# Loads for the adaLN steps from GpSimd's queue during scan and attention, and the scan's transposes one piece later

## The chip, the cores and the metric

The kernel runs on one core of a Trainium2 chip. A core has five engines that run their own instruction streams in order and wait for each other through semaphores: TensorE (PE in the profile, with its weight loads as PEld), VectorE (DVE), ScalarE (ACT), GpSimd (POOL) and SyncE (SP, which only issues DMAs). DMAs can be issued from SP, ACT and POOL; an issuing instruction stands in that engine's stream like any other, so what follows it on the same engine comes after it. The metric is the time of one execution on the device, in microseconds.

## What the reference computes

One inference step of a small hybrid network with two layers, 1024 features, 128 context tokens and 512 latent tokens, all in float32. What matters here lies in layer 0:

- adaLN: from a condition vector, `mod = silu(cond) @ w_ada + b_ada` gives shift, scale and gate for the mixer and the FFN of each layer. `w_ada` has 1024 x 6144 numbers for each of the two layers; the result is needed for two conditions (latent and context).
- the even mixer: multi-head latent attention (8 heads, softmax over 640 keys for latent tokens and 128 for context tokens) beside a gated DeltaNet scan in both directions (8 heads, chunks of 64 tokens). The scan's outputs are normalised per head, multiplied with a SiLU gate and go, beside the attention's, through one output projection.
- then SwiGLU, and layer 1 with an mLSTM mixer and another SwiGLU, which the change does not touch.

## The kernel before

The 640 tokens are held feature-major (128 features on the partitions, tokens along the row). Large matrix products are made from two parts of each weight and operand and run on PE at almost full occupancy for most of the execution. One stretch is different: from about 303 to 560 us, after the input projection of layer 0 and before its output projection. There four kinds of work are interleaved by Python generators:

- `expand` (`mla_expand`): for each tile of 128 tokens the up-projections for q, k and v (L1607), norms with a power on POOL (L1656, L1706), and two pieces later the transposes of the result (`emit_T`, L1623), copied by ACT into one staging tile `st` (L1630, one buffer) and stored from there by a DMA on SP's queue into `qTd` or `kTd` (L1632).
- `heads` (`mla_heads`): 16 blocks of two heads and 128 queries, in two pieces each: scores (L1774, L1781), row maxima on DVE (L1776, L1783), exponentials on ACT (L1787), transposes (L1791), product with v (L1804), and a factor spread on POOL (`rbc`, L1801) that a last product uses (L1806).
- `steps` (`chain`): the scan, in 20 pieces. Each two pieces are one chunk step; at its start two DMAs on SP's queue load its matrices into a tile `J` of two buffers (L1514), POOL scales the state (`S`, L1524), and PE and DVE alternate (L1540, L1555, L1565, L1577 on PE). After pieces 8 and 16 and at the end, `delta` handles the outputs of the tiles that are complete: it adds the directions (L1248), loads the gate from `gzd` by a DMA on SP's queue (L1251), squares on ACT (L1255), reduces on DVE (L1257 to L1259), takes a power on POOL (`fac`, L1261), multiplies on DVE (`on`, L1262 and L1263), transposes on PE (L1269) and multiplies the gate in from PSUM on DVE (L1270).
- `ada_more`: one adaLN step and the loads for the next. A step is four matmuls of 256 columns (L500) on one 128 x 1024 block of `w_ada`, which one DMA of 512 KB brings (L483 for the first two sixths of a layer, L486 for the rest). 52 of the 96 blocks come in earlier stages, into a tile `wa`. The other 44 are loaded in this stretch, into the three buffers `wr` that also take the large products' weights (L291). A load waits until the buffer's last reader is done: for an adaLN block that is its step on PE.

The order in the program is given by `run`, which takes one piece of the attention, one `ada_more` and one piece of the chain, over and over: 6 rounds with `expand` and 32 with `heads`, 38 in all. The chain gives way 33 times in it, so it ends in the 34th round. What is left of the adaLN steps follows behind the rounds, and in the tail two splits of the attention's and the scan's outputs feed the output projection (L371 from 560 us on).

The order on each engine is fixed before the kernel runs: a planner of the framework goes through the program with a timing model of its own and lets an engine take, among what is ready at its simulated time, what stands first in the program. What a piece issues may therefore stand earlier or later on its engine than the text of the kernel suggests, and the engines keep that order whatever the chip's real times are.

The lines that set the rounds and a load's place are these:

```python
def ada_more(s):
    if s.aw:
        s.ada_done()
        with s.tc.issue_after(s.gate.ins) if s.gate else nullcontext():
            s.ada_step(1)
    s.ada_load(2 - len(s.aw))
...
run(expand, steps, 1, 1, s.ada_more)
...
run(heads, steps, 1, 1, s.ada_more)
```

Of the kernel before, what the change touches and what calls it, by code (L numbers as in the profile page):

```python
# [214 lines left out]
class K:  # L215
# [28 lines left out]
    def c(s, n):  # L244
        gn, o, w = CONST_COLS[n]
        return s.groups[gn][:, o:o + w]
# [213 lines left out]

    def ada_init(s):
        nc = s.nc
        cs = s.t(s.base, [P, KD, 32], "cond", 1)
        nc.sync.dma_start(cs, s.I["cond"])
        s.cs = cs
        nc.scalar.activation(s.cs, cs, AF.Silu)
        s.ada = [s.t(s.base, [P, 48, 2], f"ada{l}", 1) for l in range(2)]
        s.sw = {}
# [5 lines left out]
    def ada_load(s, n):  # L474
        nc = s.nc
        while s.loads and n:
            n -= 1
            l, b, k = s.loads.pop(0)
            w = s.t(*s.wa)
            src = s.I["w_ada"][l, k]  # L480
            if b < 2:

                s.loaded = nc.sync.dma_start(w.rearrange("p (j n) -> p j n", j=2),  # L483
                                             src[:, :2048].rearrange("p (j n) -> p j n", j=2)[:, :, b * 512:(b + 1) * 512])
            else:
                s.loaded = nc.sync.dma_start(w, src[:, b * 1024:(b + 1) * 1024])  # L486
            s.aw.append(w)

    def ada_step(s, n=1):
# [357 lines left out]
def body(nc, tc, I, O, dbg=None):  # L847
    with ExitStack() as es:
        s = K(nc, tc, I, O, es, dbg)
        s.plan = plan(I)  # L850
        s.ada_init()
        s.ada_start()
        X, norm, e0 = even_mixer(s)
        x1, xw = ExitStack(), ExitStack()

        def nxt():
            return Norm(s, X, s.scale_w(1, 1, s.p("nmix")[:, 8:16]), s.vec(1, 0), s.pool("oh", 1, x1, side="right"), xw, "ow")
        norm = s.ffn(0, X, norm, e0, nxt)
        X, norm, e1 = odd_mixer(s, X, norm, x1, xw)
        s.ffn(1, X, norm, e1)  # L860
        for k in range(KD - 1):
            nc.sync.dma_start(O["yT"][:, k, :], X[:, k, :])
        for n in range(2):
            nc.sync.dma_start(O["yT"][:, KD - 1, 320 * n:320 * n + 320], X[:, KD - 1, 320 * n:320 * n + 320])


def even_mixer(s):
    nc, I, O = s.nc, s.I, s.O
# [7 lines left out]
    with ExitStack() as es:  # L876
# [16 lines left out]
        with ExitStack() as en:  # L893
# [50 lines left out]
            for n in ("qnr", "knr"):  # L944
                cw = s.t(bp, [P, 6, 32], "cw" + n, 1)
                sw = s.t(bp, [P, 6, 2, 2, 8], "sw" + n, 1)
                w = s.p(n)
# [26 lines left out]
        with ExitStack() as ec:  # L974
# [249 lines left out]
            for hf in range(2):  # L1224
# [3 lines left out]
                nc.vector.tensor_copy(SM[r, 8 + hf], K3[r, :, 0, 4])  # L1228
                nc.vector.tensor_copy(SM[r, 9 - hf], K3[r, :, 1, 4])
        s.wa = s.w, [P, 1024], "wr", WR  # L1230
        eh.close()

        US = [Bg[i // 4][:, (i % 4) * 8:(i % 4) * 8 + 8, :].rearrange("p s d -> p (s d)") for i in range(10)]
# [6 lines left out]
        def delta(ts):  # L1240

            on = {}
            for t in ts:
                o, sq = s.t(fp, [P, 512], "o", 2), s.t(fp, [P, 512], "on", 2)
                for hf in range(2):
                    r = slice(64 * hf, 64 * hf + 64)
                    sf, sb = (2 * t + hf, 7 - 2 * t - hf) if t < 4 else (8 + hf, 9 - hf)
                    nc.vector.tensor_add(o[r], US[sf][r], US[sb][r])  # L1248
                on[t] = o, sq
            for t in ts:  # L1250
                nc.sync.dma_start(zt[t].rearrange("p (b k) -> p b k", b=4), gzd[:, :, t * P:(t + 1) * P])  # L1251
            yield 1
            for t in ts:
                o, sq = on[t]
                nc.scalar.activation(sq, o, AF.Square)  # L1255
                red = s.t(fp, [P, 8], "red", 2)
                nc.vector.tensor_reduce(out=red, in_=sq.rearrange("p (s d) -> p s d", s=8), axis=AX.X, op=ALU.add)  # L1257
                nc.vector.tensor_tensor(red, red, f2[:, t, :], op=ALU.mult)
                nc.vector.tensor_scalar(red, red, 1.0 / 64 / 64, EPS, op0=ALU.mult, op1=ALU.add)  # L1259
                fac = s.t(fp, [P, 8], "fac", 2)  # L1260
                nc.gpsimd.tensor_tensor(fac, red, c("mhalf")[:, :8], op=ALU.pow)  # L1261
                nc.vector.scalar_tensor_tensor(fac, in0=fac, scalar=0.125, in1=rq[:, t, :], op0=ALU.mult, op1=ALU.mult)  # L1262
                nc.vector.tensor_tensor(sq.rearrange("p (b a d) -> p a b d", a=2, b=4), o.rearrange("p (a b d) -> p a b d", a=2, b=4),  # L1263
                                        fac.rearrange("p (a b) -> p a b", a=2).unsqueeze(3).to_broadcast([P, 2, 4, 64]), op=ALU.mult)
                yield 1
            for t in ts:
                pt = s.p1()
                for b in range(4):
                    nc.tensor.transpose(pt[:, b * P:(b + 1) * P], on[t][1][:, b * P:(b + 1) * P], c("ident"))  # L1269
                nc.vector.scalar_tensor_tensor(zt[t], in0=pt, scalar=won, in1=zt[t], op0=ALU.mult, op1=ALU.mult)  # L1270
                yield 1

        def chain(pool):
            for n, _ in enumerate(scan(s, pool, qk, SM, EGL, scr, US)):
                yield 1
                if n in (7, 15):
                    yield from delta((4,) if n == 7 else (1, 2))
            yield from delta((0, 3))
# [894 lines left out]
```

## Time and profile before

| | |
|---|---|
| median of 3 runs | 1830.22 us (1830.02 to 1830.99) |
| the profiled execution | 1834.05 us, span from first to last instruction 1832.3 us |
| mean granted clock of TensorE | 0.974 of full speed |
| busy share of the span: PE, PEld, DVE, ACT, POOL | 95%, 88%, 63%, 41%, 22% |
| HBM traffic | 115 GB/s over the span |
| stretch 303 to 560 us: busy PE, DVE, ACT, POOL | 234.68, 153.80, 107.26, 42.70 us of 257 |

The span leaves out 1.75 us of the profiled execution, which lies 3.83 us above the median of the unprofiled runs. The granted clock takes one of two levels, full speed (2.4 GHz, written 1.00) and half of it (1.2 GHz, written 0.50); a window that holds both shows a mean.

### The profile page before, as it was taken

What the parts mean: (1) busy time and instruction counts of PE and PEld (TensorE: products, weight loads), DVE (VectorE), ACT (ScalarE), POOL (GpSimd) and SP (SyncE); (2) the same over time, 40 slices, a digit from 0 to 9 for tenths busy, and PEclk for the clock granted to TensorE, in tenths of its full rate; (3) what the DMA queues carried; (4) which work ended last, traced back from release to release, by engine and by line L of the source; (5) the groups of instructions that cost most, each with busy time, mean ns of one, the idle gap of its engine ahead of it and who ended that gap; (6) DMA issues with size and microseconds to landing.
All of it is one profiled execution on the core that took longest, in us unless ns stands there. A gap on an engine that the chain in (4) does not pass through costs nothing.

```text
span 1832.3 us, 34561 instructions
## 1 busy us (share of the span) xinstructions
PE 1748.9 (95%) x14159; PEld 1615.2 (88%) x14159; DVE 1155.8 (63%) x2217; ACT 756.7 (41%) x1472; POOL 397.4 (22%) x334
## 2 busy tenths in 40 slices
PE   5999988898999989999999999999998999999999
PEld 3888877665669989999999999988998999999999
DVE  5568997465664688458538573544657873684573
ACT  3454435432434555235415343621426451452251
POOL 2026323211110124124123000022301421340330
PEclk9999997899999999999999999999999999999999
DMA  9576542785733222323312334421321232233122
GB/s 367 167 215 203 188 131 97 203 243 158 196 116 106 59 68 83 95 67 84 102 58 84 114 108 118 127 75 53 104 73 45 90 94 82 70 87 98 58 78 84
DMA packets 96163, 212.90 MB, mean 116 GB/s; under 512 B 7964, under 2 KB 41436, under 8 KB 94596
## 3 DMA queue, kind: packets, MB, share of 16 engines
q1 hardware_dynamic: 92980, 205.37, 36.4%
q10 hardware_dynamic: 3024, 5.32, 1.1%
q8 instruction: 111, 1.82, 0.4%
q14 instruction: 48, 0.39, 0.1%
HBM read 189.91 MB, written 20.75 MB: 115 GB/s over the span
## 4 chain that ended last, share of the span: by engine, by line
PE 80%; DVE 8%; DMA 5%; ACT 3%; issue 2%; SPq 1%; POOL 1%; ACTq 0%; DVEq 0%; POOLq 0%
PE mm L371 30%; PE p L352 18%; PE mm L352 12%; PE pa L500 2%; PE p L1781 2%; PE p L401 1%; PE p L1804 1%; DVE tmp L1413 1%; PE p L2044 1%; PE p L1791 1%; PE p L1607 1%; DMA wr<-in_w_ada 1%; ACT hf L789 1%; SPq L1940 1%; DMA D<-grd 1%
## 5 line engine op out<-in xcount | busy, mean ns | idle before, releaser
L286 ACT CAST wp<-wr 128x1024 fp32r<-128x1024 f32 (+2 forms) x224 | 188.0, 840 | 486.5 <-PE mm L371 350.0
L371 PE MATMUL mm<-hi,wp 128*128 128x320 f32 x1696 | 330.9, 313 | 1.5 <-DVE x L544 0.7
L287 DVE TENSOR_TENSOR wp<-wr,wp 128x1024 fp32r<-128x1024 f32 (+2 forms) x220 | 256.8, 1169 | 74.7 <-ACT wp L286 67.6
L371 PE MATMUL mm<-hf,wp 128*128 128x320 f32 x1836 | 278.7, 310 | 0.6 <-DVE x L544 0.4
L371 PEld LDWEIGHTS mm<-hi,wp 128*128 128x128 f32 x1696 | 266.6, 188 | 14.1 <-issue 8.5
L371 PEld LDWEIGHTS mm<-hf,wp 128*128 128x128 f32 x1836 | 273.2, 189 | 1.1 <-PE mm L371 1.1
L371 PE MATMUL mm<-lo,wp 128*128 128x320 f32 x848 | 196.7, 311 | 0.0
L544 DVE SCALAR_TENSOR_TENSOR x<-mm,ada,x 128x320 f32<-128x320 f32 (+2 forms) x174 | 66.2, 434 | 201.2 <-PE mm L371 191.6
L352 PE MATMUL p<-T,wp 128*128 128x320 f32 x1164 | 185.8, 308 | 0.0
L352 PEld LDWEIGHTS p<-T,wp 128*128 128x128 f32 x1164 | 174.6, 188 | 0.0
L287 DVE TENSOR_TENSOR wp<-st,wp 128x512 fp32r<-128x512 f32 x160 | 135.1, 866 | 22.7 <-ACT wp L286 21.3
L352 PE MATMUL p<-B,wp 128*128 128x320 f32 x864 | 143.9, 309 | 1.9 <-ACT wp L286 1.9
L371 PEld LDWEIGHTS mm<-lo,wp 128*128 128x128 f32 x848 | 142.2, 188 | 1.2 <-issue 0.4
L286 ACT CAST wp<-st 128x512 fp32r<-128x512 f32 x160 | 95.7, 621 | 100.3 <-PE p L352 42.8
L312 POOL TENSOR_TENSOR st<-st,wr 128x512 f32<-128x512 f32 x40 | 54.0, 1351 | 382.4 <-DMA wr<-in_w_fi 107.9
L352 PEld LDWEIGHTS p<-B,wp 128*128 128x128 f32 x864 | 131.0, 188 | 2.5 <-ACT wp L286 2.5
L352 PE MATMUL mm<-T,wp 128*128 128x320 f32 x756 | 119.9, 308 | 0.0
L352 PEld LDWEIGHTS mm<-T,wp 128*128 128x128 f32 x756 | 113.2, 187 | 0.0
L352 PE MATMUL mm<-B,wp 128*128 128x320 f32 x576 | 95.4, 309 | 0.9 <-ACT wp L286 0.9
L352 PEld LDWEIGHTS mm<-B,wp 128*128 128x128 f32 x576 | 87.3, 188 | 1.2 <-ACT wp L286 1.2
L312 POOL TENSOR_TENSOR st<-wr,st 128x512 f32<-128x512 f32 x40 | 69.9, 1747 | 6.9 <-DVE wp L287 6.2
L623 POOL TENSOR_TENSOR a<-a,p 128x320 f32<-128x320 f32 x40 | 37.9, 948 | 145.7 <-DVE p L584 144.6
(511 smaller groups left out, 2818.1 us busy)
## 6 DMA issues: line engine op xcount, KB each, us to landing
wr<-in_w_fi SPq DMA_DIRECT2D x68, 512.0 KB, 3.6
wa<-in_w_ada SPq DMA_DIRECT2D x52, 512.0 KB, 5.6
wr<-in_w_ada SPq DMA_DIRECT2D x44, 512.0 KB, 4.5
wr<-in_w_fo SPq DMA_DIRECT2D x32, 512.0 KB, 3.5
wr<-in_w_odd SPq DMA_DIRECT2D x25, 512.0 KB, 3.6
wr<-in_w_even SPq DMA_DIRECT2D x22, 512.0 KB, 4.9
J<-scr SPq DMA_DIRECT2D x20, 512.0 KB, 7.6
w<-in_w_fi SPq DMA_DIRECT2D x20, 512.0 KB, 3.6
```

The costliest lines, as they stand in the source:

```text
L286: s.nc.scalar.copy(hi, raw)
L287: (eng or s.nc.vector).tensor_tensor(lo, raw, hi.bitcast(F32), op=ALU.subtract)
L312: eng.tensor_tensor(whole[f], x, y, op=op)
L352: s.nc.tensor.matmul(out, a[:, k, :], op(k, n, p), start=(k == 0 and q == 0 and not onto), stop=(k == nk - 1 and q == 2), skip_group_check ...
L371: s.nc.tensor.matmul(ps[:, n, :320], a[:, k, :], op(k, n, p), start=(k == 0 and q == 0), stop=(k == nk - 1 and q == 2))
L401: s.nc.tensor.matmul(o, a[:, k, :], op(k, n, p), start=(k == 0 and q == 0), stop=(k == nk - 1 and q == 2))
L500: nc.tensor.matmul(ps[32 * g:32 * g + 32, :256], s.cs[:, k, :], w[:, g * 256:(g + 1) * 256], start=(k == 0), stop=(k == KD - 1))
L544: s.nc.vector.scalar_tensor_tensor(x[:, a:b], in0=ps[:, a - 320 * n:b - 320 * n], scalar=gate[:, k, i:i + 1], in1=x[:, a:b], op0=ALU.mult, ...
L623: nc.gpsimd.tensor_tensor(a1, a1, p5, op=ALU.mult)
L789: nc.scalar.activation(b_[:, r], t[:, r], AF.Identity, bias=s.sh[:, o, i:i + 1], scale=s.sw[:, o, i:i + 1])
L1413: nc.vector.tensor_tensor(tv, x[:, j, j + 1:].unsqueeze(2).to_broadcast(sh), x[:, j, :m].unsqueeze(1).to_broadcast(sh), op=ALU.mult)
L1781: nc.tensor.matmul(sa, qT[:, a, t, :], kf[:, a, :512], start=True, stop=True)
```

## The change

Two things are changed. First, a handle `s.wq` names the engine whose queue issues the adaLN loads. It is SP at the start, and GpSimd from the place on where the loads begin to use the `wr` buffers, ahead of `expand`. So all 44 loads of the stretch are issued from POOL's stream; blocks, sizes, buffers and the program's order of the loads stay. No other DMA moves.

Second, `delta` gives way once more, between its factors and its transposes. Each of the three calls has one more piece, and in each one more round of attention and `ada_more` stands in the program between the last `on` (L1263) and the first transposes (L1269). The chain gives way 36 times then and ends in round 37 of 38. Everything behind a `delta` in the chain comes one piece later for each call.

```diff
     def ada_init(s):
         nc = s.nc
+        s.wq = nc.sync
         cs = s.t(s.base, [P, KD, 32], "cond", 1)
...
             if b < 2:
 
-                s.loaded = nc.sync.dma_start(w.rearrange("p (j n) -> p j n", j=2),
+                s.loaded = s.wq.dma_start(w.rearrange("p (j n) -> p j n", j=2),
                                              src[:, :2048].rearrange("p (j n) -> p j n", j=2)[:, :, b * 512:(b + 1) * 512])
             else:
-                s.loaded = nc.sync.dma_start(w, src[:, b * 1024:(b + 1) * 1024])
+                s.loaded = s.wq.dma_start(w, src[:, b * 1024:(b + 1) * 1024])
             s.aw.append(w)
...
         s.wa = s.w, [P, 1024], "wr", WR
+        s.wq = s.nc.gpsimd
         eh.close()
...
                                         fac.rearrange("p (a b) -> p a b", a=2).unsqueeze(3).to_broadcast([P, 2, 4, 64]), op=ALU.mult)
                 yield 1
+            yield 1
             for t in ts:
                 pt = s.p1()
```

## Rows read from the trace of the kernel before

**Rows 1.** The page: span, and the chain that ended last by engine.

```profile
span 1832.3 us, 34561 instructions
...
PE 80%; DVE 8%; DMA 5%; ACT 3%; issue 2%; SPq 1%; POOL 1%; ACTq 0%; DVEq 0%; POOLq 0%
```

**Rows 2.** Windows: us, busy time of each engine (instructions), PE clock, DMA share, GB/s.

```profile
303.00:560.00 257.00, 234.68 (x3116) 161.78 (x3114) 153.80 (x450) 107.26 (x291) 42.70 (x51) 0.94 0.60 171
```

**Rows 3.** Waits of PE, 303 to 560 us: waiter, releaser, us in total, times, longest.

```profile
PE pa L500 <- DMA wr<-in_w_ada: 7.9, 6, 4.0
PE p L1269 <- DVE on L1263: 4.1, 1, 4.1
PE p L1623 <- ACT st L1630: 3.4, 1, 3.4
```

**Rows 4.** Timeline around the first transposes: start, us, engine, line, [idle before and releaser].

```profile
415.80 1.64 POOL L1261 TENSOR_TENSOR fac<-red,consts 128x8 f32<-128x8 f32 x1 [9.25 <-DVE red L1259]
...
418.51 1.09 PE L1269 MATMUL p<-consts,on 128*128 128x128 f32 x4 [4.12 <-DVE on L1263]
...
419.39 1.92 PE L1781 MATMUL p<-kT,qT 128*128 128x512 f32 x2
...
421.24 1.13 PE L1540 MATMUL p<-S,qk 64*64 64x64 f32 x32
...
422.30 1.22 PE L1774 MATMUL p<-kT,qT 128*128 128x128 f32 x4
...
423.31 1.25 PE L1781 MATMUL p<-kT,qT 128*128 128x512 f32 x2
```

**Rows 5.** Timeline: the same kinds of instruction at full clock, near 540 us.

```profile
537.38 0.62 PE L500 MATMUL pa<-wr,cond 128*32 128x256 f32 x4 [1.72 <-DMA wr<-in_w_ada]
...
540.09 0.66 PE L1269 MATMUL p<-consts,on 128*128 128x128 f32 x4
...
540.58 0.61 PE L1774 MATMUL p<-kT,qT 128*128 128x128 f32 x4
...
541.02 1.02 PE L1781 MATMUL p<-kT,qT 128*128 128x512 f32 x2
```

**Rows 6.** Timeline near 341 us, full clock: first scan product of a step.

```profile
341.17 0.69 PE L1540 MATMUL p<-S,qk 64*64 64x64 f32 x32 [2.05 <-DMA S<-in_s]
```

**Rows 7.** Windows of 5 us around the waits: columns as in rows 2.

```profile
340.00:345.00 5.00, 3.83 (x40) 3.12 (x41) 1.88 (x6) 2.35 (x4) 2.78 (x3) 0.69 1.03 236
...
355.00:360.00 5.00, 5.00 (x62) 3.14 (x58) 1.87 (x7) 1.04 (x2) 1.64 (x1) 0.50 0.52 137
...
415.00:420.00 5.00, 1.49 (x5) 1.25 (x6) 1.51 (x5) 0.00 (x0) 1.64 (x1) 0.69 0.98 213
420.00:425.00 5.00, 5.00 (x54) 2.80 (x52) 2.35 (x7) 1.12 (x4) 0.00 (x0) 0.62 0.10 18
...
535.00:540.00 5.00, 3.28 (x35) 1.97 (x32) 1.79 (x5) 1.24 (x3) 1.85 (x3) 1.00 0.75 281
```

**Rows 8.** Waits on SP's own queue, 303 to 560 us.

```profile
SPq L486 <- PE pa L500: 90.6, 19, 23.4
SPq L1514 <- PE p L1577: 19.0, 6, 6.8
```

**Rows 9.** Issues of the 44 blocks: duration ns min/median/max; time to landing, min/median/max.

```profile
L486 SPq DMA_DIRECT2D wr<-in_w_ada x32: 327/335/1307, 372.7 to 534.6; - x32
...
DMA to landing us min/median/max: 3.6/4.5/11.7
```

**Rows 10.** The chain that ended last, 295 to 560 us: loads and stores in it.

```profile
341.27 10.85 DMA kTd<-st
...
484.52 6.89 DMA wr<-in_w_ada
...
531.16 6.18 DMA wr<-in_w_ada
```

**Rows 11.** POOL's instructions in the stretch: xcount, busy us, mean ns, idle before.

```profile
L1706 POOL TENSOR_TENSOR rsq<-redq,consts 128x8 f32<-128x8 f32 x6 | 9.8, 1640 | 21.3 <-DVE redq L1704 21.3
```

## The prediction

> **What bounds the kernel now.** I read the page first. The chain that ended last runs through PE for 80% of the span [rows 1], so time is won only where PE stands idle or runs at the lower clock. Next I asked for the windows of the stretch that the change touches, 303 to 560 us: PE is busy for 234.68 of 257 us at a mean clock of 0.94, the DMA engines for 0.60, POOL for 42.70 us [rows 2]. So 22 us of idle PE, and what the half clock costs, are all that can be won here; POOL has 214 us to spare. Which idle time it is stands in PE's waits [rows 3]: six waits of the adaLN matmuls (L500) for their blocks, 7.9 us together, one wait of 4.1 us of the scan's transposes (L1269) for `on`, and one of 3.4 us of the attention's transposes (L1623) for ACT. The reader is to see that both parts of the change point at a row of this short list.
>
> The timeline around the longest of these waits [rows 4] shows why it comes: the power on POOL alone takes 1.64 us, and PE stands for 4.12 us in front of L1269. Then L1781, L1540, L1774 and L1781 follow, none of which reads `on`. They take nearly twice as long as their like near 540 us or 341 us [rows 5, 6], because the granted clock fell: the windows have 0.69 and 0.62 there, against 1.00 elsewhere [rows 7]. So that wait costs more than its length.
>
> SP's queue is the last view. Loads of blocks stood there for 90.6 us in 19 waits for PE, the longest 23.4 us, with whatever came behind them; but the loads of `J` waited 19.0 us for PE themselves, for the readers of their buffer (L1577) [rows 8]. Taking the blocks away frees the issue of few of them.
>
> **The change part by part.** *The transposes one piece later.* No instruction is added; 20 matmuls move back on PE. In front of the first four now stand one more piece of attention and one more adaLN step: L1781 1.02, L1774 0.61 and L500 0.62 us [rows 5], together 2.25 us of the 4.12 (other ready work, such as the 0.69 us of L1540 [rows 6], I leave uncounted). A wait of 1.87 us stays. Whether the clock still falls then is between two rows: behind a wait of 1.72 us it stayed at 1.00, behind one of 2.05 us its window has 0.69 [rows 5 to 7]. 1.87 is slightly nearer to the first, so I count the clock as kept. That gives back the differences of the five rows: 0.43 for L1269, 0.90 and 0.23 for L1781, 0.44 for L1540, 0.61 for L1774 [rows 4 to 6], 2.61 us. The part wins 2.25 + 2.61 = 4.86 us; its bounds are 0 (the planner keeps the order) and 4.12 + 2.61 = 6.73. The other two calls win nothing: PE has no second wait of L1269 for DVE [rows 3]. What is late next is the gate's product on DVE and, at the end, the split of `zt`; the chain ends in round 37 of 38, so the last round covers it, at no price. Without that cover it would be one piece, some 257/38 = 6.8 us.
>
> *The loads on POOL: the issue.* SP spent a median of 0.335 us on one [rows 9]; no DMA is issued from POOL in this trace. The nearest rows are that 0.335 us below and POOL's slowest repeated operation, the power of 1.640 us, above [rows 11]; I take 1.0, midway. For 44 loads this is 44 us of POOL, hidden in its 214 idle us [rows 2]. Queued behind a load are POOL's powers (L1706, L1261), its scaling of `S` and `rbc`, and DVE and PE wait for those; the load itself waits for PE's last step on its buffer, an earlier place in PE's order, so such waits should be short. What shows is lateness: 0.67 us at each of the six waits of L500, which have no slack, a loss of 4.0 us (bounds 0 and 6 x 1.31 = 7.9).
>
> *The loads on POOL: the queue they leave.* On SP a block goes behind the `J` and gate loads issued just before it. At 484.52 and 531.16 us the chain holds blocks of 6.89 and 6.18 us [rows 10], against a median of 4.5 to landing [rows 9]. If a queue of their own takes them to the median, 2.39 + 1.68 = 4.07 us come back, and the waits there are long enough to show it (bounds 0 and 4.07). This I take whole.
>
> *What stays on SP.* The store of `st` at 341.27 us took 10.85 us [rows 10] in a stretch where the DMA engines are full, 1.03 at 236 GB/s [rows 7], and the wait of 3.4 us at L1623 hangs on it [rows 3]. A block of 512 KB at that rate takes 2.2 us. One block goes ahead of this burst on SP today and one behind the store; on POOL they trade places with it in part, so I take 0 with bounds of 2.2 us either way.
>
> The Trainium skill bears on this in "DMA: Bandwidth & Descriptors", section "Queues, rings and completion order": each DMA engine takes turns, packet by packet, between the queues that have work. The rows of this trace have only loads in one queue, where the later block lands behind the store, and no run here shows the sharing. By the rule the block behind the store would take its 2.2 us ahead of it, and the sum would lose that; by the rows alone it loses nothing.
>
> The sum: -4.86 + 4.0 - 4.07 + 0 = -4.9 us. The profiled execution of 1834.05 us would become 1829.1. It lies 3.83 us above the median of the runs; taken from that median, 1830.22 - 4.9 = 1825.3 us.
>
> **The rivals.** *The loads start late (slower).* Place: POOL, in front of the six waits of L500. Blocks are loaded in groups as buffers come free, so a block can find another load or a power before it. With 1.64 us for its own issue and half of another 1.64 in front, less SP's 0.335, each is 2.1 us late; six waits cost 12.8 us, and no shorter way in the queue gives any back: 1830.22 - 4.86 + 12.8 = 1838.1. It decides the sign from (4.86 + 3.66)/6 = 1.4 us of lateness per wait. For it: the six waits have no slack, and no row tells POOL's price. Against it: POOL is idle for five sixths of the stretch. Chance 0.24.
>
> The Trainium skill would make this rival worse: "SBUF — State Buffer", section "SBUF: two separate sides", says that GpSimd writes the descriptors of its DMAs itself and cannot while some VectorE operations hold the port that the two share, so that such a load waits for VectorE. DVE is busy for 153.80 of the 257 us [rows 2], but no row here shows a load from POOL, held up or not.
>
> *The store pays.* The turn-taking above, worked out from rows as a mechanism of this kernel: a block takes 2.2 us of the full DMA engines from the store at 341.27, L1623 and with it PE stand that much longer: 1825.3 + 2.2 = 1827.5. For it: DMA share 1.03 [rows 7]; against it: the earlier block no longer leads the burst. Chance 0.16.
>
> *The store gains.* The same trade the other way: the store lands 2.2 us earlier, the wait of 3.4 us [rows 3] shrinks below 1.72 us, and the clock, 0.50 behind it in 355 to 360 us [rows 7], stays up: 2.2 + 2.5 us for that window alone, and 1.2 for what more is left of the wait: 1825.3 - 5.9 = 1819.4. Chance 0.10.
>
> *The transposes don't move, or another wait takes their place.* The planner takes what is ready by its own times and may put L1269 where it was, or the filling may stall on DVE in its turn. Then the 4.86 us are not won and the loads cancel: 1830.2. For it: PE's order is not the program's. Chance 0.12.
>
> **How the numbers follow.** The forecast keeps 0.38, with a range of its own of 1821 to 1829. A measurement of this kernel tells about 0.2% from no change, 3.66 us: faster is below 1826.56, slower above 1833.88. Faster: 0.30 of the forecast, 0.03 of the paying store, all 0.10 of the gaining one, 0.01 of the unmoved transposes, 0.44. Slower: 0.19 of the late loads, 0.01 of the paying store, 0.02 of the unmoved transposes, 0.22. The same: what is left, 0.34. The range goes from 1818 to 1838: below it lies part of the gaining store (0.04), above it the worse half of the late loads (0.13).
>
> **What would show it.** In the profile after: SP has no issue of `in_w_ada` left behind 300 us, POOL has 44, each about 1 us apart where they come in a group. PE's waits list L1269 with under 2 us, and the windows at that place have a clock above 0.9. The waits of L500 for its blocks sum to about 8 us again, but the blocks land in about 4 to 5 us also behind `J` loads. The store of `st` in the burst still takes about 11 us. The prediction is wrong if L500 waits 15 us or more, if L1623 waits 5 us, if L1269 waits as before, or if DVE and PE now wait for POOL's powers or `rbc`; a change of the planned order elsewhere that costs or gives more than these would also break it.

## The result, and the profile after

The change makes the kernel slower: 1849.16 us (median of 4 runs, 1845.39 to 1855.48) against 1830.61 us for the kernel before beside it, a ratio of 1.0095, 95% interval [1.0076, 1.0114]. Two repeats further down give 1.0061 [1.0045, 1.0077] and 1.0081 [1.0061, 1.0102]. The range of the prediction ended at 1838.0 us. The profiled execution of the changed kernel took 1850.27 us. Its lines have moved by 1 to 3 numbers: L500 is now L501, L1263 is L1265, L1269 is L1272, L1623 is L1626, L1540 is L1543, L1781 is L1784, and the blocks are issued at L484 and L487.

The page, first and fourth part, beside [rows 1]:

```profile
span 1848.5 us, 34586 instructions
...
PE 74%; DVE 9%; issue 6%; DMA 6%; ACT 3%; SPq 1%; POOL 1%; ACTq 0%; DVEq 0%; POOLq 0%
```

The stretch, which ends at 572.9 us in place of 560.5, and the window that holds the first transposes; columns as in [rows 2]:

```profile
303.00:573.00 270.00, 244.07 (x3111) 163.69 (x3111) 155.01 (x452) 106.56 (x291) 67.40 (x94) 0.94 0.60 164
...
425.00:430.00 5.00, 2.63 (x32) 1.75 (x36) 1.15 (x3) 0.00 (x0) 1.67 (x1) 1.00 0.89 170
```

The waits of PE in it, beside [rows 3]:

```profile
PE pa L501 <- DMA wr<-in_w_ada: 13.6, 6, 6.1
PE p L1558 <- DVE r L1547: 2.5, 1, 2.5
PE p L1794 <- ACT pp L1790: 2.4, 4, 1.1
PE p L1272 <- DVE on L1265: 2.3, 1, 2.3
```

The stretch is 12.4 us longer, but PE's busy time in it grew by 9.4 us (244.07 against 234.68), at the same mean clock. That is the riddle of this case: most of the loss is not a wait. The wait of the transposes did shrink, from 4.12 to 2.26 us, and in this profile the clock there stays at 1.00, as the timeline shows (beside [rows 4]):

```profile
425.08 1.67 POOL L1263 TENSOR_TENSOR fac<-red,consts 128x8 f32<-128x8 f32 x1 [1.11 <-DVE red L1261]
...
427.83 0.63 PE L1272 MATMUL p<-consts,on 128*128 128x128 f32 x4 [2.26 <-DVE on L1265]
...
428.74 1.02 PE L1784 MATMUL p<-kT,qT 128*128 128x512 f32 x2
```

The clock did not stay up each time. In the two repeats of the changed kernel (e5, e16) the wait is 2.26 us again, but the clock is at half from 424.7 to 428.1 us and from 430.7 to 434.1 us, at or just behind the wait. In e16:

```profile
431.00 1.09 PE L1272 MATMUL p<-consts,on 128*128 128x128 f32 x4 [2.26 <-DVE on L1265]
...
432.74 1.73 PE L1784 MATMUL p<-kT,qT 128*128 128x512 f32 x2
```

The wait of 3.4 us for ACT's `st` is gone from the list. The six waits for blocks grew from 7.9 to 13.6 us, though. The chain in the stretch now holds these loads of blocks, beside [rows 10]:

```profile
337.71 11.14 DMA wr<-in_w_ada
...
451.09 8.16 DMA wr<-in_w_ada
497.50 9.12 DMA wr<-in_w_ada
555.07 6.20 DMA wr<-in_w_ada
```

The issues of the 44 blocks and their landing, beside [rows 9] (there the trace tells the landing of 34 of the 44 only):

```profile
L487 POOL DMA_DIRECT2D wr<-in_w_ada x32: 527/528/601, 372.8 to 555.1; - x32
L484 POOL DMA_DIRECT2D wr<-in_w_ada x12: 722/748/955, 310.8 to 371.9; - x12
...
DMA to landing us min/median/max: 3.9/5.0/14.3
```

**The block that lost its place.** The longest of the waits is one event, and the timeline tells it. Before:

```profile
334.20 0.38 SPq L483 DMA_DIRECT2D wr<-in_w_ada  x1
...
336.36 3.65 SPq L1514 DMA_DIRECT2D J<-scr  x4
...
338.48 0.64 PE L500 MATMUL pa<-wr,cond 128*32 128x256 f32 x8 [0.52 <-DMA wr<-in_w_ada]
```

After:

```profile
337.60 2.56 SPq L1517 DMA_DIRECT2D J<-scr  x4
337.71 0.75 POOL L484 DMA_DIRECT2D wr<-in_w_ada  x1 [1.78 <-PE pa L501]
...
348.89 1.08 PE L501 MATMUL pa<-wr,cond 128*32 128x256 f32 x8 [6.11 <-DMA wr<-in_w_ada]
```

On SP the block stood in front of the four `J` loads of the scan's first step (2 MB) and had 2.2 us on them; PE waited 0.52 us. From POOL it is issued 0.11 us after the first of them, lands after 11.14 us, and PE waits 6.11 us. Behind it the clock is at half from 347.9 to 354.8 us (the matmul takes 1.08 us in place of 0.64).

**Work that is not a wait.** The timeline of PE in the changed kernel, only the adaLN matmuls, all at full clock. Each matmul shows as two records, so a step of four is x8:

```profile
409.91 0.62 PE L501 MATMUL pa<-wr,cond 128*32 128x256 f32 x2
411.10 0.64 PE L501 MATMUL pa<-wr,cond 128*32 128x256 f32 x8
...
415.96 0.63 PE L501 MATMUL pa<-wr,cond 128*32 128x256 f32 x4
...
435.53 0.63 PE L501 MATMUL pa<-wr,cond 128*32 128x256 f32 x6
...
444.07 1.05 PE L501 MATMUL pa<-wr,cond 128*32 128x256 f32 x10
...
450.12 1.07 PE L501 MATMUL pa<-wr,cond 128*32 128x256 f32 x16
```

One matmul takes as long as four, and five as long as eight. The four matmuls of a step write to different 32 columns of the array and run side by side, if nothing of another kind stands between them. Counted from a run's first record to the next kind's start, one matmul alone holds PE for 0.55 us, a whole step for 0.57, two steps in a row for 1.00, three for 1.43: about 0.15 us for each run and 0.425 for each pass of up to four. A step that is broken in two costs 0.57 us more. The Trainium skill names the cause in "TensorEngine Tiling (Array Packing)", section "Tiling Modes": changing the tiling mode, not only the tile, drains TensorE; the rows agree with it.

The planner breaks steps where something else is ready. In the planned order of the kernel before, the 176 adaLN matmuls of the stretch stand in 41 runs, which make 55 passes of up to four; in the changed kernel in 52 runs and 60 passes, 3.8 us more by that price; the traces have the same runs and passes. Changes from any kind of matmul to another in the planned order, which the expectations below go by, rose from 355 to 383.

Another count tells more. The timeline prints the part of the array that a matmul uses (`128*128`, `128*96`, `128*64`, `128*32`, `64*64`, `32*32`), its shape. From the two matmuls `mm<-th,consts` ahead of the stretch (at 252.8 us in the kernel before) to the output projection, PE goes from one shape to another 266 times in the kernel before and 296 times in the changed one. PE's own work over the same instructions is the time from each matmul's start to the next one's, less the idle time before that next one, where a matmul at half clock is valued at its kind's mean at full clock. It is 251.2 us before, and 258.6, 258.9 and 257.5 us in the three profiles of the changed kernel. Over all 18 profiles (table below) it grows by 0.27 us for each change of shape; a straight line through them misses by 0.9 us as a rule and by 2.6 us at most (e11). A step broken in two, two changes more, costs 0.57 us, which agrees. The count was made after the runs, and no run varies it alone.

### The profile page after: what moved, and what is told of

It is laid out like the page before. It is cut to its first block, busy times and chain, and to the rows that moved or that the text cites. A ratio compares the mean times of both kernels' runs of the same rounds, so it can differ in the third digit from the quotient of the medians.

```text
span 1848.5 us, 34586 instructions
## 1 busy us (share of the span) xinstructions
PE 1761.3 (95%) x14159; PEld 1621.1 (88%) x14159; DVE 1158.7 (63%) x2217; ACT 756.7 (41%) x1472; POOL 420.7 (23%) x378
## 4 chain that ended last, share of the span: by engine, by line
PE 74%; DVE 9%; issue 6%; DMA 6%; ACT 3%; SPq 1%; POOL 1%; ACTq 0%; DVEq 0%; POOLq 0%
PE mm L371 28%; PE p L352 18%; PE mm L352 12%; DMA wr<-in_w_ada 2%; PE pa L501 2%; PE p L1610 1%; PE p L1784 1%; DVE tmp L1416 1%; PE p L2047 1%; PE p L1807 1%; DVE X L1417 1%; PE p L2051 1%; PE p L1794 1%; ACT hf L790 1%; PE p L401 1%
```

## The experiments

Each was timed beside the kernel before. "At full clock" is the span times its mean granted clock, averaged over the runs, and "clock" what is left of the span: a us at half clock counts as half a us lost. The next column is the number of changes of kind in PE's planned order of the stretch; the last two, changes of shape and PE's work, are read from each run's one profile.

| run | edit | median us | ratio, 95% interval | at full clock | clock | changes of kind | of shape | PE's work, us |
|---|---|---|---|---|---|---|---|---|
| before | | 1830.6 to 1832.1 | | 1782.8 | 47.3 | 355 | 266 | 251.2 |
| changed, e5, e16 | both parts | 1849.2, 1843.8, 1847.8 | 1.0095, 1.0061, 1.0081 | 1796.3 | 48.8 | 383 | 296 | 258.6, 258.9, 257.5 |
| e1 | loads from POOL alone | 1841.5 | 1.0048 [1.0027, 1.0070] | 1787.2 | 51.9 | 362 | 271 | 252.3 |
| e2 | later transposes alone | 1836.6 | 1.0020 [1.0002, 1.0038] | 1787.4 | 46.8 | 368 | 285 | 255.9 |
| e3 | later, loads from ACT | 1837.5 | 1.0030 [1.0014, 1.0046] | 1789.3 | 46.3 | 371 | 288 | 255.2 |
| e4 | later, POOL from `heads` on | 1841.1 | 1.0047 [1.0031, 1.0063] | 1790.6 | 48.0 | 380 | 292 | 257.0 |
| e6 | extra piece elsewhere, but the same program as e2 | 1839.8 | 1.0034 [1.0018, 1.0049] | 1788.7 | 48.5 | 368 | 285 | 256.4 |
| e7 | later in one call of three | 1836.6 | 1.0024 [1.0007, 1.0042] | 1787.4 | 48.4 | 353 | 281 | 254.5 |
| e8 | POOL from `heads` on alone | 1838.2 | 1.0033 [1.0020, 1.0047] | 1786.3 | 51.0 | 359 | 267 | 251.3 |
| e9, e15 | two pieces fewer | 1829.0, 1828.9 | 0.9986, 0.9983 | 1780.2 | 47.3 | 344 | 265 | 250.3, 250.5 |
| e10 | loads from ACT alone | 1840.1 | 1.0038 [1.0022, 1.0054] | 1791.4 | 45.9 | 355 | 281 | 255.0 |
| e11 | adaLN steps in pairs | 1836.3 | 1.0024 [1.0011, 1.0036] | 1783.1 | 51.7 | 350 | 269 | 248.5 |
| e12 | four pieces fewer | 1838.0 | 1.0051 [1.0033, 1.0069] | 1785.1 | 51.9 | 372 | 274 | 252.0 |
| e13 | seven pieces fewer | 1849.1 | 1.0108 [1.0087, 1.0130] | 1787.6 | 60.1 | 351 | 263 | 249.4 |
| e14 | e9 with pairs | 1833.3 | 1.0020 [1.0007, 1.0034] | 1782.3 | 49.9 | 333 | 264 | 249.4 |

The changed kernel loses 13.5 us at full clock and 1.5 us to the clock. Its executions, and those of nearly all variants, scatter by 3 to 5 us (standard deviation), those of the kernel before by 2.5; single profiles are read with that in mind.

### Which part costs

**e1**, `delta` as before:

```diff
-            yield 1
             for t in ts:
                 pt = s.p1()
```

> All 44 loads from POOL, the transposes where they were before. Theory A (the loads cost the time: blocks land late through a queue of their own and POOL's stream; the later transposes give about 2 us back): 1847 to 1853 us, the six waits of PE for blocks 13 us or more, the wait for `on` 4 us again. Rival B (the later transposes and the order planned round them cost it, the loads are neutral): 1828 to 1833 us, waits for blocks near 8 us.

1841.51 us, so the loads do cost (rival B falls), but some 9.5 us and not the 15 or more of theory A; what the changed kernel loses beyond that must lie with the other part. PE's own work hardly grew (252.3 against 251.2 us): the loss lies in waits and in the clock, 4.4 us at full clock and 4.6 to the clock. Waits of PE in the stretch, and the timeline of the block:

```profile
PE pa L501 <- DMA wr<-in_w_ada: 19.1, 8, 8.6
PE p L1271 <- DVE on L1265: 5.8, 1, 5.8
```

```profile
334.98 0.75 POOL L484 DMA_DIRECT2D wr<-in_w_ada  x1 [1.60 <-PE pa L501]
335.05 2.46 SPq L1516 DMA_DIRECT2D J<-scr  x4
...
347.12 1.08 PE L501 MATMUL pa<-wr,cond 128*32 128x256 f32 x8 [8.65 <-DMA wr<-in_w_ada]
```

Here the block is issued 0.07 us ahead of the first `J`, and it still takes 12.1 us: what it lost is the place in one queue, not the time of issue. POOL's first packet of 4 KB starts at 336.94 us and the first `J` packet of 8 KB at 337.25 us, and the block's last packet at 345.42 us. The DMA view of 334 to 341 us (queue: packets, MB, share of the 16 engines) shows POOL's queue q0 and SP's q1 at work together:

```profile
q1 hardware_dynamic: 948, 1.30, 65.9%
q0 software_dynamic: 104, 0.41, 26.8%
```

**e2**, loads on SP:

```diff
-        s.wq = s.nc.gpsimd
+        s.wq = s.nc.sync
```

> The transposes one piece later, all 44 loads on SP as before. Theory A: 1826 to 1830 us (the wait for `on` shrinks from 4.1 to about 2 us and the clock stays up). Rival B: 1843 us or more.

1836.62 us, between the two and nearer to a loss: neither theory. PE waits less than before for blocks and for `on`:

```profile
PE pa L501 <- DMA wr<-in_w_ada: 5.7, 5, 1.7
...
PE p L1272 <- DVE on L1265: 1.3, 1, 1.3
```

Still the kernel is 5 us slower, and 4.6 us slower at full clock. So the later transposes cost outside the waits: PE's work is 255.9 us in place of 251.2, with 19 more changes of shape, which at 0.27 us each would make 5.1 us. The clock is at half here too, from 422.4 to 425.8 us, behind a wait of 1.27 us:

```profile
422.21 0.92 PE L1272 MATMUL p<-consts,on 128*128 128x128 f32 x4 [1.27 <-DVE on L1265]
```

**e5 and e16**, the changed kernel again:

> The changed kernel once more, beside the three that follow, since its own median rests on four executions. If the two parts add up (+10.0 us for the loads alone, +5.1 for the transposes alone) its median is near 1846 us; if they make each other worse, 1849 us or more; if the four executions were high by chance, 1841 us or less.

> The changed kernel a third time, beside it, so that its loss is measured with as many executions as the others. From ten executions so far: 1843 to 1849 us.

1843.75 and 1847.84 us. The parts alone cost 9 to 10 us (e1) and 5 to 8 us (e2 and its repeat e6, below); together 12 to 19 us. They add up within the scatter.

### Where the loads cost

**e4**, loads on SP during `expand`, and **e8**, the same without the later transposes:

```diff
-        s.wq = s.nc.gpsimd
...
+        s.wq = s.nc.gpsimd
         run(heads, steps, 1, 1, s.ada_more)
```

> As the changed kernel, but the loads go on SP during `expand` and from POOL only from `heads` on (after about 375 us). If the cost is that of the crowded stretch of `expand` (a block of 11.1 us at 337.7 us, PE standing 6.1 us for it), the time is 1830 to 1836 us; if it is spread over the whole stretch, 1839 to 1845 us; if it is all in the attention and scan behind 375 us, 1847 us or more.

> No extra piece; loads on SP during `expand`, from POOL only from `heads` on. If the ten microseconds of the loads alone come from the one block that lost its place ahead of the `J` loads in `expand` (12.1 us to landing, PE standing 8.7 us), this is 1830 to 1834 us. If POOL's stream costs all along, 1836 us or more.

1841.12 and 1838.16 us. In e8 SP issues seven blocks, the last at 347.6 us, and POOL the others from 354.6 us on. The waits for blocks fall to 8.7 us (longest 3.3) and 6.0 us (longest 3.9): the one wait of 6 to 9 us is gone, and it stood in all four profiles with POOL's loads during `expand` (6.1, 8.7, 9.1 and 8.6 us). That is about 3 us of e1's 10 and some 6 of the changed kernel's. The rest of the loads' cost isn't the lost block. In e8 it is 3.5 us at full clock and 3.7 us by the clock, and its profile shows no wait that grew by as much (`on` 5.8 against 4.1 us), nor more work of PE (251.3 against 251.2 us). POOL's own stream does not show it either: of the five powers `fac` none starts more than 0.9 us behind the `red` that it needs, except behind another power. Where e8's time goes stays open.

**e3**, ACT in place of POOL, and **e10**, the same without the later transposes:

```diff
-        s.wq = s.nc.gpsimd
+        s.wq = s.nc.scalar
```

> As the changed kernel, but the 44 loads issued from ACT. Theory A1 (what hurts is that blocks no longer stand in one queue with the `J`, gate and store transfers, and share the DMA engines with them): 1845 to 1852 us as in the changed kernel, waits for blocks of 13 us and landings up to 14 us. Theory A2 (what hurts is POOL: its slow issue, and its powers, `S` and `rbc` behind loads that wait): the waits for POOL's work vanish, 1826 to 1836 us unless ACT's exponentials wait behind the loads in their turn, which would show as waits of PE for `pp` well over the 2.4 us of the changed kernel.

> Loads from ACT, no extra piece; 355 changes of kind as before. If a queue of their own is what costs the loads from POOL their ten microseconds, 1838 to 1843 us. If it is POOL, 1830 to 1835 us. Rival F gives 1834 to 1840 us for this kernel too, so only a result under 1834 or over 1840 us decides.

1837.51 and 1840.14 us. With the later transposes ACT's queue costs 1 us more than SP's (e2). That misses theory A1 by 7.5 us and A2 by 1.5 us, and lies nearer to A2: a queue of their own costs little there, while POOL's costs 9 us more (1846.5 us, the median of the changed kernel's 16 executions), some 3 of them PE's work (258 against 255.2 us). Without the later transposes ACT's queue costs 8 us, but 1840.14 us stands at the bound of 1840 us, so by its own expectation e10 does not decide. Nor does it vary the queue alone: PE's order was planned anew, with 281 changes of shape in place of 266, though the count of kinds stayed at 355, and PE's work is 255.0 us, 3.8 more than before. That is half of e10's loss of 8 us; its waits for blocks are 8.2 us, as before, and the other half is not found, since the one profile is of the fastest execution (1829.47 us). In e3 the order is nearly e2's (288 changes against 285), and so is the work (255.2 against 255.9 us). So whether POOL's queue or any queue of their own makes the loads dear is not shown.

In e10 the block of `expand` is issued at 336.30 us, behind all four `J` loads, and takes 12.2 us too. At first it took no turns: for 6 us, until 342.42 us, no packet of ACT's queue moved. Then both queues had packets, here from 341 to 348 us (ACT's is q10):

```profile
q1 hardware_dynamic: 652, 1.02, 62.0%
q10 hardware_dynamic: 380, 0.75, 37.6%
```

e3 shows the same: the block is issued at 338.08 us and has its first packet at 344.07 us. PE waits 5.1 us for it there, and 1.3 us in e10.

### Where the later transposes cost

**e6**, the extra piece at the head of `delta`, and **e7**, the later transposes in the first call alone; loads on SP in both:

```diff
         def delta(ts):
 
+            yield 1
             on = {}
```
```diff
-            yield 1
+            if ts == (4,):
+                yield 1
             for t in ts:
```

> Loads on SP; the extra piece stands at the head of each `delta`, ahead of its additions, and the transposes follow their products as before. The chain has as many pieces as with the later transposes. Theory C (what costs is that the chain ends three rounds later and PE's planned order changes with it): 1835 to 1841 us, as the later transposes alone or worse by the wait for `on` of 4 us. Rival D (it is the transposes' own new place): 1829 to 1833 us.

> Loads on SP; the extra piece only in the first of the three calls of `delta`, where the trace of before has its wait of 4.1 us. If the part's gain was real there and the two other calls cost it, 1825 to 1829 us. If any shift of the chain against attention and adaLN costs through the order, 1832 to 1837 us.

1839.81 and 1836.59 us. The planner made the same program of e6 as of e2: every instruction of every engine is the same, in the same order. So e6 is a second measurement of e2, 3.2 us higher, and does not test the transposes' place: theory C and rival D stay undecided between them. With one piece or with three, 4.6 to 5.9 us are lost at full clock. e7 speaks against the count of kinds: it has 353, fewer than before, and loses as much. The count of shapes agrees with its loss: it has 281 changes, 15 more than before, and PE's work grew by 3.3 us. Its adaLN steps are broken up as in e2 (58 passes, 45 runs), and its waits for blocks are as before (8.3 us).

**e9 and e15**, one piece for two transposed tiles, a shift the other way:

```diff
                 nc.vector.scalar_tensor_tensor(zt[t], in0=pt, scalar=won, in1=zt[t], op0=ALU.mult, op1=ALU.mult)
-                yield 1
+            yield 1
```

> A control that goes the other way: loads on SP, no extra piece, and in `delta` the two transposed tiles share one piece instead of two, so the chain is two pieces shorter than before. PE's planned order has 344 changes from one kind of matmul to another in the stretch, where the kernel before has 355 and the changed one 383. Theory E (time without waits and without the clock's share follows the number of changes of kind, about 0.25 us each): 1827 to 1831 us. Rival F (the order of the kernel before is a good one by itself, and any shift loses some 4 us): 1834 to 1840 us.

> The kernel whose `delta` gives way once for two transposed tiles (two pieces shorter, loads on SP) a second time, because its first interval ends at 0.9999. If it is really faster, the median is again 2 to 4 us under that of before and the interval stays below 1; if not, within 1.5 us of before.

1829.03 and 1828.86 us, ratios 0.9986 [0.9972, 0.9999] and 0.9983 [0.9969, 0.9997]: this beats both kernels by a little, twice, with 2.6 us less at full clock, though both intervals end just under 1. Rival F falls. The two longest entries of PE's waits in e15 are no shorter than before, and PE's work is 250.5 us in place of 251.2:

```profile
PE pa L501 <- DMA wr<-in_w_ada: 9.0, 8, 3.8
PE p L1271 <- DVE on L1265: 4.1, 1, 4.1
```

**e12 and e13**, more pieces taken out of `delta` (e9's edit, and behind the factors; e12 has the line with the plus, e13 neither):

```diff
                                         fac.rearrange("p (a b) -> p a b", a=2).unsqueeze(3).to_broadcast([P, 2, 4, 64]), op=ALU.mult)
-                yield 1
+            yield 1
```

> Loads on SP; in `delta` both of the per-tile pieces of the factors and of the transposes share one piece, so the chain is four pieces shorter than before. PE's planned order has 372 changes of kind in the stretch, against 355 before and 368 with the one later piece alone. Theory E (PE's own work grows with each change of kind and with each adaLN step that is broken up): 1834 to 1838 us. Rival L (what costs is how late the chain ends): 1825 to 1829 us, below the 1829.0 us of the chain that is two pieces shorter.

> Loads on SP; `delta` gives way only twice, after its loads and at its end, so the chain is seven pieces shorter than before. The planned order has 351 changes of kind, and the adaLN steps fall into 52 passes of four matmuls instead of 55. Theory E: 1828 to 1832 us, since the wait of the transposes for `on` grows while PE's work falls by some 3 us. Rival L: 1822 us or less.

1837.98 and 1849.10 us. Rival L falls: a chain that ends sooner isn't faster by that. Theory E misses e13 by 17 us. e13 shows the other side of the trade, PE's wait for `on`, five times, where before it came once:

```profile
PE p L1270 <- DVE on L1265: 14.0, 5, 4.0
```

It has the highest loss to the clock of all, 60.1 us. e12 came out as theory E said, but hardly for its reason: PE's work rose by 0.8 us only, while the `on` waits are 6.5 us in 3 (4.1 before) and the clock takes 4.6 us more.

**e11 and e14**, two adaLN steps in every second round (e14 with e9's edit):

```diff
-        if s.aw:
+        s.tick = 1 - s.tick
+        if s.tick and s.aw:
             s.ada_done()
             with s.tc.issue_after(s.gate.ins) if s.gate else nullcontext():
-                s.ada_step(1)
+                s.ada_step(2)
```

> Loads on SP, no extra piece; two adaLN steps stand together in every second round in place of one in each, 37 runs of adaLN matmuls on PE in place of 41, 350 changes of kind. Theory E: 1828 to 1831 us if the blocks are there in time, since a block is asked for earlier ahead of its use. Rival F: 1834 us or more.

> Loads on SP, the chain two pieces shorter, and two adaLN steps together in every second round: 333 changes of kind, 50 passes. PE's work without waits should be some 5 us under that of the kernel before. Theory E with waits for blocks as in the kernel with pairs alone: 1829 to 1833 us; with the waits of the kernel before: 1825 to 1829 us.

1836.34 and 1833.33 us, both misses. The price of a broken step is borne out: e11 has 37 runs in 49 passes and should save 3.2 us of PE; PE's work fell by 2.7 us in its profile. But PE's idle time rose by 4.3 us between the first of these adaLN steps and the output projection, and the clock takes 4.4 us more. Less work on PE is no gain where it opens waits.

## Why the prediction was wrong

**The transposes.** The wait shrank about as predicted, to 2.26 us (1.87 forecast) in all three profiles and to 1.27 in e2. The clock, 2.61 of the 4.86 us, was kept in one profile of the changed kernel and fell in its two repeats and in e2. The two rows that the prediction chose between do not decide it: it fell behind 1.27 us and stayed behind 2.26. (Two of the four matmuls that it calls nearly twice as long, 1.13 us against 0.69 and 1.25 against 1.02, are less than that; the sum uses the right differences.) The step that failed is "No instruction is added; 20 matmuls move back on PE", with the sum of 4.86 us put on it: it takes PE's other work as fixed. A change of the planned order elsewhere stands last among the prediction's signs of being wrong, with no price and no chance. Shown: the extra pieces change the planned order (e2, which e6 repeats, and e7), and PE's own work grows by 3 to 5 us, by more than the waits gain. By the price above the adaLN runs make 2.2 us of it in e2 (41 runs and 55 passes against 47 and 58); counted with all other changes of shape, 19 in e2 and 15 in e7, the growth of 4.7 and 3.3 us comes out at 5.1 and 4.0. That these changes are the cause is argued from the count over all profiles. The last round "at no price" was true of waits only.

**The issue on POOL.** As forecast, SP has no issue of a block left in the stretch and POOL has 44. Over-sized was the price: a median of 0.53 us for 32 of them and of 0.75 for the other 12, against 1.0. The Trainium skill's "SBUF — State Buffer", section "SBUF: two separate sides", would have such an issue stand while VectorE holds the shared port; the longest in this trace is 0.96 us against the median of 0.75, so at most a fifth of a us shows.

**The queue they leave.** This failed by its sign. "If a queue of their own takes them to the median, 2.39 + 1.68 = 4.07 us come back": the median rose from 4.5 us (of 34 blocks) to 5.0, and the block in front of `J` went from 4.2 us to 11.1; the slowest, 14.3 us at 374.5 us, is another. The place in front of `J` was an asset that the sum left out: it had looked at blocks behind `J` alone. The turn-taking that the prediction weighed for the store ("DMA: Bandwidth & Descriptors" of the Trainium skill, section "Queues, rings and completion order") is seen in e1's two queues. It struck the block, 4.2 us to 12.1, and the store a little, 10.85 us to 11.4. With ACT's queue, packets took no turns for the first 6 us.

**The store.** It landed in 8.7 us in the first profile of the changed kernel, and in 12.5 and 11.9 us in the two repeats, against 10.85 before. So the rival that saw it gain was right in one profile of three, by luck, and the one that saw it pay in two, with 1.6 and 1.0 us of its 2.2. L1626's wait vanished in all three, but the block's wait of 6 to 9 us stands in front of the same place now.

**The slower rival** had the direction and the place, the six waits of L501, but another mechanism: no load stood long in POOL's queue for a power; one lost its place, and that wait alone is 6 of the 13.6 us (9 of 15.3 and of 16.7 in the repeats).

**The sum.** The pieces, forecast at -4.86 us, measure +5 to +8 alone; the loads, forecast at 4.0 - 4.07, measure +9 to +10 alone. What remains open: the 6 us that e8 loses with no wait and no work of PE to show for them, the half of e10's 8 us that is not PE's work, and with both, what POOL's queue costs beyond the one block.

## What to carry to other kernels

Before a piece is moved in a program that a planner orders, compare the planned orders of both kernels: how often PE goes from one shape of the array to another, and how many steps of narrow matmuls are broken up, for that is work that no list of waits shows. Compare them for every experiment too: an edit meant to move a queue can move PE's order (e10), and one meant to move the order can leave the program as it was (e6). A transfer's place in a queue can be an asset: look for what stands behind it before it is given a queue of its own. And where a gain is one wait of four us, time enough executions to see five us the other way.

## What the hardware showed unexpectedly

- A 32-column matmul of 256 columns alone holds PE for 0.55 us, four on different columns together 0.57 us. A change from one shape of the array to another goes with 0.27 us of PE's work over 18 profiles.
- An issue of 512 KB from POOL takes 0.53 us in rows of 4 KB and 0.75 us in two runs of 2 KB for each partition; the median to landing is 5.0 us, against 4.5 from SP (of 34 of the 44).
- In the burst POOL's packets ran among SP's from the first `J` packets on (e1); ACT's stood for 6 us first (e3, e10) and ran among SP's then.
- Behind a wait of 2.26 us of PE in the same place the granted clock stayed at 1.00 once and was 0.50 twice; behind one of 1.27 us in e2 it was 0.50.
